# A two-layer hybrid decoder on one core: compressed keys and values in alternating row groups, a norm's weights spread by transpositions, and a new order of the work

## The chip, the core and the metric

The kernel runs on one NeuronCore of a Trainium2 chip. The core has five engines with instruction lists of their own: TensorE (PE in the profile; its weight loads are PEld), VectorE (DVE), ScalarE (ACT), GpSimd (POOL) and SyncE (SP), which here only issues DMAs. The metric is the device time of one execution in microseconds (us). Runs of the kernel before took 556.07, 558.59 and 560.09 us; their median is 558.59.

## What is computed

Two layers of a decoder with 512 tokens and 1024 channels, in float32. Each layer normalises its input, multiplies it by one wide matrix, feeds the columns to four mixers (A: attention on the best 128 keys that an indexer finds; B: attention on compressed, selected and windowed keys with gates; C: a short gated convolution; D: pooling over several windows), gates the results, multiplies them by an output matrix and adds the input. A last normalisation ends it. Cut to what the change touches:

```python
def hybrid_layer(x, norm_w, w_in, w_out, conv_w, pe_cmp, w_cmp_k, w_cmp_v, pool_w, pool_scale):
    h = rmsnorm(x, norm_w)
    p = split_cols(h @ w_in)
    ...
    return x + mixed @ w_out

def compress(tok, w):
    blocks = tok[:, cmp_idx] + pe_cmp
    return blocks.reshape(B, n_cmp, CMP_LEN * HEAD_DIM) @ w

k_cmp = rope(compress(kc_tok, w_cmp_k)[:, :, None], cmp_end, ROT_DIM)[:, :, 0]
v_cmp = compress(vc_tok, w_cmp_v)
```

Compression makes 31 (padded to 32) short keys and values of 64 channels, each from 32 tokens.

## The kernel before

The tokens are four tiles of 128. For the layer's first product, `norm_tile` (line 729) normalises a tile on VectorE, transposes it on TensorE and splits it into a high and a low part (hT, copied by ScalarE and VectorE). Weights come in quarters of 256 rows (`load_w`, line 558): a DMA into a staging tile (st), a cast to the high part (wh) and a subtraction for the low part (wl). A product of hidden state and weights is then three MATMULs per 128 channels (high by high, high by low, low by high), so one tile and one group of columns take 24 (`lin_tok`, line 592). The first group of columns (360) of all four tiles takes 96.

Attention (`probs`, line 995, and `pv`, line 1029) makes scores of four heads on TensorE, takes the smallest on VectorE, exponentials on ScalarE, sums and inverses on VectorE, scales the probabilities on GpSimd, transposes them on TensorE (tr<-ident,pb) and multiplies them by the values.

The work isn't issued as it is written. `record` (line 266) puts every operation on a tape, `cost` (line 318) gives it a duration, the time for which its engine is taken and the time until others see it, and `schedule` (line 388) then builds the five lists: of the operations that could start soonest on an engine it takes the one whose stage has the lowest number in the table RANK (line 195). COLD is the time up to which TensorE's operations are counted double, START the time at which an engine begins. `play` issues the lists; since all instructions are issued by one line of it, the profile names nearly all of them L513, and one goes by the names of the tiles.

Three places matter here.

- The start. `spread` (line 654) multiplies a row of ones with the first norm's weights (g_row, one partition), so that two PSUM banks hold them on all 128 partitions. `warm` (line 646) gives TensorE 40 transpositions of the identity (tr<-ident) that nobody reads; the scheduler uses them as fillers. The loads of the input, the weights and the constants all go through SP's queue.
- `compressed` (line 955) multiplies 32 rows of windows by the weights for keys (s = 0) and then for values (s = 1), 16 products each, into columns 0 to 63 and 64 to 127 of the same 32 partitions of a bank. The profile calls them tr<-st,u. The values' high part is kept in vc on partitions 0 to 31, its low part beside it, and a second copy on 32 to 63.
- The end of layer 0, where the last softmax blocks, the output product and the next layer's normalisation meet.

```python
            pc = bank("tr", 3)
            for s in range(2):
                for t in range(16):
                    PE.matmul(pc[0:32, s * HD : (s + 1) * HD], us[s][:, t::16], wts[2 * s + t // 8][:, t % 8, :],
                              start=t == 0, stop=t == 15)
```

Of the kernel before, what the change touches and what calls it, by code (L numbers as in the profile page):

```python
# [18 lines left out]
P = 128  # L19
T = 512  # L20
NT = T // P
DM = 1024
# [156 lines left out]
class Op:  # L179
    __slots__ = ("eng", "name", "args", "kw", "outs", "ins", "before", "left", "behind", "dur", "occ", "seen",  # L180
                 "tiles", "start", "ready", "num", "locks", "moves", "stage", "rank", "group")


class Engine:
# [9 lines left out]
START = {"PE": 0, "DVE": 0, "ACT": 2070, "POOL": 750, "SP": 800}  # L194
RANK = [
# [28 lines left out]
]  # L224
COLD = 6000


class Tape:
# [1099 lines left out]
```

## Time and profile before

| | |
|---|---|
| runs | 556.07, 558.59, 560.09 us |
| the profiled execution | 558.61 us, its span 556.9 us |
| TensorE busy | 536.8 us of the span |
| VectorE, ScalarE, GpSimd busy | 420.4, 320.4, 294.8 us |
| DMA | 50.62 MB, 91 GB/s over the span |

The span runs from the first to the last instruction; the time holds 1.7 us more. A line of a timeline gives the start in us, the length of the merged piece, the engine, the operation, the tile written <- the tiles read, its shape, how many instructions were merged, and in brackets the idle time of the engine before it with what released it. SPq is the queue of DMAs that SyncE issues. MATMULs are pipelined, so the length of one holds its way through the array, and the distance of two starts says what each costs in a row.

### The profile page before, as it was taken

The page shows a single profiled execution, that of the slowest core. Times are in us where ns is not written, and L with a number is a line of the kernel's source. Part 1 is how long each engine was busy: PE and PEld are TensorE (multiplying, and loading weights), DVE is VectorE, ACT ScalarE, POOL GpSimd, SP SyncE. Part 2 cuts the span into 40 slices and gives each one's busy share as a digit, 9 for nine tenths or more (in the row PEclk, how much of TensorE's full clock was granted, in tenths as well). Part 3 has the DMA queues.
Part 4 walks back from the last instruction along what each step waited for, and adds up shares of the span by engine and source line. Part 5 has one row for each costly group of instructions (what it writes and reads, how often), then busy time and mean ns, then how long its engine had stood idle before and what let it go on. Part 6 is the DMA issues. An engine that isn't in the chain of part 4 may idle for free.

```text
span 556.9 us, 9669 instructions
## 1 busy us (share of the span) xinstructions
PE 536.8 (96%) x3092; PEld 462.2 (83%) x3092; DVE 420.4 (75%) x1152; ACT 320.4 (58%) x797; POOL 294.8 (53%) x399
## 2 busy tenths in 40 slices
PE   8999999999999999899999999999999998999995
PEld 6899987787788778678999999778878876879895
DVE  3837889999998777863256677989999889797623
ACT  4557865443575658563445777555547556776523
POOL 4465743474284746443754666329352583753622
PEclk9999999999999999999999999999999999999998
DMA  8942310583121112106752433148131421030204
GB/s 265 270 127 57 77 39 20 146 202 89 38 76 30 57 39 75 28 2 179 213 156 73 114 92 73 48 111 205 46 87 28 115 55 50 0 106 1 95 1 151
DMA packets 70084, 50.62 MB, mean 91 GB/s; under 512 B 19217, under 2 KB 64401, under 8 KB 70034
## 3 DMA queue, kind: packets, MB, share of 16 engines
q1 hardware_dynamic: 69890, 49.76, 32.5%
q8 instruction: 24, 0.39, 0.3%
q10 hardware_dynamic: 144, 0.26, 0.1%
q14 instruction: 26, 0.21, 0.1%
HBM read 45.81 MB, written 4.19 MB: 90 GB/s over the span
## 4 chain that ended last, share of the span: by engine, by line
PE 75%; DVE 8%; ACT 5%; DMA 4%; POOL 3%; issue 2%; SPq 1%; POOLq 0%; ACTq 0%; DVEq 0%
PE mm L513 56%; PE tr L513 9%; PE s L513 6%; PE pv L513 4%; DMA st<-in_w_in_dram 2%; POOL wl L513 2%; DVE cd L513 2%; SPq L513 1%; DVE acc L513 1%; DVE pb L513 1%; ACT wh L513 1%; DVE pl L513 1%; DMA x<-in_x_dram 1%; ACT qiT L513 1%; ACT rl L513 1%
## 5 line engine op out<-in xcount | busy, mean ns | idle before, releaser
L513 POOL TENSOR_TENSOR wl<-st,wh 128x768 fp32r<-128x768 f32 (+4 forms) x94 | 159.0, 1705 | 77.6 <-ACT wh L513 71.3
L513 PE MATMUL mm<-hT,wh 128*128 128x512 f32 x544 | 179.8, 402 | 1.9 <-ACT wh L513 0.8
L513 PEld LDWEIGHTS mm<-hT,wh 128*128 128x128 f32 x544 | 99.5, 188 | 21.9 <-ACT wh L513 3.8
L513 PE MATMUL mm<-wh,hT 128*128 128x360 f32 (+3 forms) x480 | 104.5, 308 | 0.9 <-ACT z L513 0.9
L513 PE MATMUL mm<-hT,wl 128*128 128x512 f32 x272 | 102.8, 398 | 0.0
L513 POOL TENSOR_SCALAR pb<-pb,rs 128x512 f32<-128x512 f32 (+3 forms) x96 | 55.7, 597 | 78.1 <-DVE rs L513 68.0
L513 ACT ACTIVATE wh<-st 128x768 fp32r<-128x768 f32 (+4 forms) x92 | 71.0, 778 | 40.5 <-PE mm L513 21.8
L513 PE MATMUL mm<-wh,mT 128*128 128x384 f32 (+1 forms) x384 | 92.2, 324 | 1.7 <-ACT wh L513 0.9
L513 PEld LDWEIGHTS mm<-wh,hT 128*128 128x128 f32 x480 | 78.6, 189 | 2.0 <-ACT z L513 1.5
L513 PEld LDWEIGHTS mm<-wh,mT 128*128 128x128 f32 x384 | 66.2, 189 | 5.2 <-ACT wh L513 1.7
L513 PE MATMUL mm<-wl,hT 128*128 128x360 f32 (+3 forms) x240 | 69.8, 307 | 0.3 <-POOL wl L513 0.2
L513 ACT ACTIVATE pb<-pb,mn 128x256 f32<-128x256 f32 (+3 forms) x96 | 53.4, 558 | 25.8 <-DVE mn L513 25.6
L513 PE MATMUL mm<-wl,mT 128*128 128x384 f32 (+1 forms) x192 | 58.8, 323 | 0.0
L513 PEld LDWEIGHTS mm<-hT,wl 128*128 128x128 f32 x272 | 51.0, 188 | 8.9
L513 DVE MAX8 m<-acc 128x8 f32<-128x384 f32 (+2 forms) x96 | 51.7, 551 | 0.5
L513 DVE MATCH_REPLACE8 acc<-m,acc 128x256 f32<-128x256 f32 (+2 forms) x96 | 51.9, 542 | 0.2
L513 ACT ACTIVATE ph<-tr 128x512 fp32r<-128x512 f32 (+1 forms) x68 | 37.7, 593 | 18.8 <-PE tr L513 18.4
L513 DVE TENSOR_TENSOR pl<-tr,ph 128x512 fp32r<-128x512 f32 x60 | 40.2, 684 | 8.3 <-ACT ph L513 7.6
L513 PEld LDWEIGHTS mm<-wl,hT 128*128 128x128 f32 x240 | 44.3, 189 | 1.2 <-POOL wl L513 1.0
L513 PE MATMUL tr<-ident,pb 128*128 128x128 f32 x240 | 44.0, 274 | 1.2 <-POOL pb L513 1.1
L513 DVE CUSTOM_DVE_ANT_0 pb<-s,mask 128x128 f32<-128x128 f32 (+3 forms) x72 | 32.8, 464 | 14.9 <-PE tr L513 7.5
L513 PEld LDWEIGHTS tr<-ident,pb 128*128 128x128 f32 x240 | 30.5, 140 | 11.3 <-POOL pb L513 4.1
(157 smaller groups left out, 898.0 us busy)
## 6 DMA issues: line engine op xcount, KB each, us to landing
st<-in_w_in_dram SPq DMA_DIRECT2D x104, 128.0 KB, 2.6
st<-in_w_in_dram SPq DMA_DIRECT2D x28, 256.0 KB, 3.1
st<-in_w_out_dram SPq DMA_DIRECT2D x16, 384.0 KB, 3.3
x<-in_x_dram SPq DMA_DIRECT2D x16, 256.0 KB, 4.6
st<-in_w_in_dram SPq DMA_DIRECT2D x8, 320.0 KB, 4.6
st<-in_w_out_dram SPq DMA_DIRECT2D x8, 256.0 KB, 2.8
x1d<-x SPq DMA_DIRECT2D x8, 256.0 KB, 4.2
x<-x1d SPq DMA_DIRECT2D x8, 256.0 KB, 3.3
```

The lines of the kernel that those rows point to most:

```text
L513: getattr(self.engines[op.eng].real, op.name)(*[real(a) for a in op.args], **{k: real(v) for k, v in op.kw.items()})
```

## The change

- Keys and values of the compression go to two groups of partitions, 0 to 31 and 32 to 63, in the same columns of one bank, and their products alternate; the weights' loads alternate likewise, and the copies of the values swap their partitions.
- The first norm's weights are loaded as eight rows of 128 by ScalarE's queue, transposed to a column per 128 channels, copied by VectorE, and each column, repeated 128 times, is transposed again into its place in the two banks. The row of ones is gone.
- The scheduler's costs are fitted anew (the landing of a load by rows, TensorE's times, a new time `load` for which a weight load keeps the next TensorE operation away, half the time for products of 32 rows), and writes to one bank by different accumulations wait for one another only where their partitions overlap.
- All ranks are new, COLD is 5600 instead of 6000, ScalarE begins at 800 instead of 2070.

```diff
-START = {"PE": 0, "DVE": 0, "ACT": 2070, "POOL": 750, "SP": 800}
+START = {"PE": 0, "DVE": 0, "ACT": 800, "POOL": 750, "SP": 800}
 RANK = [
-    38, 15, 584, 424, 40, 0, 95, 100, 96, 43, 85, 52, 82, 97, 370, 60, 0, 585, 339, 563, 291, 0, 6, 526, 21, 73,
...
+    583, 29, 585, 581, 518, 0, 283, 160, 177, 3, 101, 151, 129, 145, 507, 102, 0, 68, 584, 582, 532, 0, 74, 105,
...
-COLD = 6000
+COLD = 5600
...
-                    for other in v.tile.groups.values():
-                        if other is not op.group:
+                    for (a, b, _), other in v.tile.groups.items():
+                        if other is not op.group and a < r1 and r0 < b:
                             op.before.update((o.num, o) for o in other)
...
-            op.seen = 2000 + rows * max(run, 512) / 240.0
+            op.seen = 2000 + rows * (2.1 + run / 685.0)
+            if op.eng == "ACT" and not any(o.eng == "ACT" for o in self.ops):
+                op.occ = 1650
         elif op.eng == "PE":
             m = int(np.prod(out.shape[1:]))
+            op.load = 109 * int(np.prod(op.args[1].shape[1:])) / 128
             if op.name == "transpose":
-                op.occ = 108 if m >= 96 else 60
-                op.seen = op.occ + 262
+                op.occ = 60
+                op.seen = 370
...
-                    op.occ = 1.75 * m - 20
+                    op.occ = 1.72 * m + 7
                     op.seen = op.occ + 270
+                    if out.shape[0] == 32:
+                        op.occ *= 0.55
...
+            if e == "PE" and last[e] is not None:
+                s = max(s, last[e].start + op.load * (2 if last[e].start < COLD else 1))
...
-    g_row = res.tile([1, DM], F32, name="g_row", tag="sga")
-    SP.dma_start(g_row, norm_w[0:1, :])
-    ones = res.tile([1, P], F32, name="ones", tag="sgb")
-    G.memset(ones, 1.0)
+    g_row = res.tile([KC, P], F32, name="g_row", tag="sga")
+    S.dma_start(g_row, norm_w[0].rearrange("(k p) -> k p", p=P))
...
     def spread():
+        pg = bank("tr", 3)
+        PE.transpose(pg[:, 0:KC], g_row, ident[0:KC, 0:KC])
+        g_col = res.tile([P, KC], F32, name="g_col", tag="sgb")
+        V.tensor_copy(g_col, pg[:, 0:KC])
         g = [bank("s", 2) for _ in range(2)]
-        for b in range(2):
-            PE.matmul(g[b], ones, g_row[:, half(b)], start=True, stop=True)
+        for k in range(KC):
+            PE.transpose(g[k // 4][:, k % 4 * P : (k % 4 + 1) * P], g_col[:, k : k + 1].to_broadcast([P, P]), ident)
         return g
...
-            for wsrc in (w_cmp_k, w_cmp_v):
-                for q in range(2):
+            for q in range(2):
+                for wsrc in (w_cmp_k, w_cmp_v):
...
-            for s in range(2):
-                for t in range(16):
-                    PE.matmul(pc[0:32, s * HD : (s + 1) * HD], us[s][:, t::16], wts[2 * s + t // 8][:, t % 8, :],
+            for t in range(16):
+                for s in range(2):
+                    PE.matmul(pc[32 * s : 32 * s + 32, 0:HD], us[s][:, t::16], wts[2 * (t // 8) + s][:, t % 8, :],
                               start=t == 0, stop=t == 15)
...
-            S.activation(vc[0:32, 0:HD], pc[0:32, HD:P], AF.Copy)
-            lo(V, vc[0:32, HD:P], pc[0:32, HD:P], vc[0:32, 0:HD])
-            S.activation(vc[32:HD], f(vc[0:32]), AF.Copy)
+            S.activation(vc[32:HD, 0:HD], pc[32:HD, 0:HD], AF.Copy)
+            lo(V, vc[32:HD, HD:P], pc[32:HD, 0:HD], vc[32:HD, 0:HD])
+            S.activation(vc[0:32], f(vc[32:HD]), AF.Copy)
```

What the new order is like shows at three places. First, TensorE's list at the start, in the kernel before (s is the bank with the spread weights, xn a normalised half-tile, tr_94 the fillers):

```order
L513 MATMUL tr_94<-ident 128x128 x16
L513 MATMUL s_154<-g_row,ones 128x512
L513 MATMUL s_168<-g_row,ones 128x512
L513 MATMUL tr_177<-ident,xn_165 128x128 x4
L513 MATMUL tr_94<-ident 128x128 x6
L513 MATMUL tr_199<-ident,xn_184 128x128 x4
L513 MATMUL tr_94<-ident 128x128 x14
L513 MATMUL tr_239<-ident,xn_203 128x128 x4
```

and in the changed kernel (tr_127 are the fillers, tr_125 the small transposition of g_row):

```order
L521 MATMUL tr_125<-ident,g_row 128x8
L521 MATMUL tr_127<-ident 128x128 x3
L521 MATMUL s_141<-ident,g_col 128x128 x4
L521 MATMUL s_157<-ident,g_col 128x128 x4
L521 MATMUL tr_127<-ident 128x128 x6
L521 MATMUL tr_181<-ident,xn_164 128x128 x4
L521 MATMUL tr_127<-ident 128x128
L521 MATMUL tr_191<-ident,xn_174 128x128 x4
L521 MATMUL tr_127<-ident 128x128 x9
L521 MATMUL mm_219<-wh_188,hT_194 128x360 x2
```

The two one-row products are replaced by nine transpositions at the head of the list, the sixteen fillers that stood ahead of them come later, and the first product of hidden state and weights moves ahead of the second tile's transpositions.

Second, SP's queue, in the kernel before (x are half-tiles of the input, st weight quarters in two pieces):

```order
L513 DMA x_79<-in_x_dram 128x512
L513 DMA x_87<-in_x_dram 128x512
L513 DMA g_row<-in_norm_w_dram 1x1024
L513 DMA x_104<-in_x_dram 128x512
L513 DMA x_113<-in_x_dram 128x512
L513 DMA x_121<-in_x_dram 128x512
L513 DMA x_132<-in_x_dram 128x512
L513 DMA st_141<-in_w_in_dram 128x2x320
L513 DMA st_141<-in_w_in_dram 128x2x40
L513 DMA st_152<-in_w_in_dram 128x2x320
L513 DMA st_152<-in_w_in_dram 128x2x40
L513 DMA st_158<-in_w_in_dram 128x2x320
```

and in the changed kernel, where x_81 and x_85 are tile 1, x_92 and x_98 tile 0, x_150 and x_159 tile 3, x_168 and x_178 tile 0 once more for the residual, x_186 and x_197 tile 2, and g_121 half of the next norm's weights:

```order
L521 DMA st_102<-in_w_in_dram 128x2x320
L521 DMA st_102<-in_w_in_dram 128x2x40
L521 DMA g_121<-in_norm_w_dram 128x512
L521 DMA st_137<-in_w_in_dram 128x2x320
L521 DMA st_137<-in_w_in_dram 128x2x40
L521 DMA x_150<-in_x_dram 128x512
L521 DMA x_159<-in_x_dram 128x512
L521 DMA x_168<-in_x_dram 128x512
L521 DMA x_178<-in_x_dram 128x512
L521 DMA x_186<-in_x_dram 128x512
L521 DMA x_197<-in_x_dram 128x512
L521 DMA st_209<-in_w_in_dram 128x2x320
```

The first weight quarter is in fifth place instead of eighth, and the residual's loads stand ahead of tile 2 and of the third quarter. The fourth follows behind one more load. On GpSimd's list the fills and masks of the constants (mask, cbias, cval, pw, u) now stand ahead of the two instructions that make the identity.

Third, TensorE's list at the end of layer 0, where the scores of the last head of group A's third tile (s_2993 in the kernel before) stand thus,

```order
L513 MATMUL s_2993<-kTA_523,qa_601 128x384
L513 MATMUL s_2993<-kTA_551,qa_601 128x384
L513 MATMUL s_3003<-kTA_523,qa_710 128x512
L513 MATMUL pv_2980<-ph_3001,vB_812 128x512
L513 MATMUL s_3003<-kTA_551,qa_710 128x512
L513 MATMUL pv_2980<-pl_3006,vB_812 128x512
L513 MATMUL tr_3017<-ident,pb_2938 128x128
L513 MATMUL tr_3019<-ident,pb_2938 128x128
```

with the block's other ten transpositions behind these two; and in the changed kernel (the last head is s_2950):

```order
L521 MATMUL s_2950<-kTA_496,qa_790 128x384
L521 MATMUL s_2950<-kTA_513,qa_790 128x384
L521 MATMUL s_2963<-kTA_496,qa_662 128x512
L521 MATMUL s_2963<-kTA_513,qa_662 128x512
L521 MATMUL tr_2970<-cd_2896,pw 128x512
L521 MATMUL mm_2883<-wh_2973,mT_2147 128x256
L521 MATMUL mm_2883<-wh_2973,mT_2151 128x256
L521 MATMUL mm_2883<-wh_2973,mT_2147 128x256
L521 MATMUL mm_2883<-wh_2973,mT_2151 128x256
L521 MATMUL tr_2986<-ident,pb_2904 128x128
L521 MATMUL tr_2988<-ident,pb_2904 128x128
L521 MATMUL mm_2990<-wh_2806,mT_2147 128x256
```

The transpositions of the probabilities no longer stand in one row of twelve: they come in groups of two to four with products of the output matrix (mT) between them, and one more score block and the pooling's product stand ahead of them.

## Rows read from the trace of the kernel before

**Rows 1.** The page, busy times by engine and the clock in 40 slices.

```profile
PE 536.8 (96%) x3092; PEld 462.2 (83%) x3092; DVE 420.4 (75%) x1152; ACT 320.4 (58%) x797; POOL 294.8 (53%) x399
...
PEclk9999999999999999999999999999999999999998
```

**Rows 2.** The chain that ended last: its last long piece.

```profile
522.63 28.05 PE mm L513 x190
```

**Rows 3.** Timeline of the start, all engines.

```profile
1.36 0.28 POOL L513 TENSOR_SCALAR_AFFINE_SELECT ident<-ident 128x128 f32<-128x128 f32 x1
...
1.70 3.67 PE L513 MATMUL tr<-ident 128*128 128x128 f32 x16 [1.70 <-POOL ident L513]
...
2.11 0.53 POOL L513 MEMSET mask<- 128x512 f32 x1
...
4.20 0.53 POOL L513 MEMSET pw<- 128x512 f32 x1
...
5.30 3.78 PE L513 MATMUL s<-g_row,ones 1*128 1x512 f32 x4
5.45 0.55 POOL L513 TENSOR_TENSOR ss<-ss,mhalf 128x1 f32<-128x1 f32 x1
...
7.49 0.75 DVE L513 SCALAR_TENSOR_TENSOR xn<-x,ss,s 128x512 f32<-128x512 f32 x1 [7.49 <-PE s L513]
...
8.08 0.63 ACT L513 ACTIVATE junk<-x 128x512 bf16<-128x512 f32 x1 [0.76 <-DMA x<-in_x_dram]
...
9.12 2.07 DVE L513 SCALAR_TENSOR_TENSOR xn<-x,ss,s 128x512 f32<-128x512 f32 x3 [0.88 <-PE s L513]
...
12.05 2.77 PE L513 MATMUL tr<-ident 128*128 128x128 f32 x14
...
14.63 0.90 DVE L513 TENSOR_TENSOR wl<-st,wh 128x720 fp32r<-128x720 f32 x1
14.66 0.60 PE L513 MATMUL tr<-ident,xn 128*128 128x128 f32 x4
...
15.67 0.90 PE L513 MATMUL mm<-wh,hT 128*128 128x360 f32 x4
16.11 0.53 DVE L513 CAST wh<-st 128x720 fp32r<-128x720 f32 x1
...
25.65 0.69 DVE L513 TENSOR_TENSOR hT<-tr,hT 128x512 fp32r<-128x512 f32 x1 [0.47 <-ACT hT L513]
```

**Rows 4.** Timeline of TensorE at the end of the first 96 products.

```profile
34.27 0.33 PE L513 MATMUL mm<-wl,hT 128*128 128x360 f32 x1
34.44 0.49 PE L513 MATMUL mm<-wh,hT 128*128 128x360 f32 x2
34.77 0.33 PE L513 MATMUL mm<-wl,hT 128*128 128x360 f32 x1
34.93 0.93 PE L513 MATMUL mm<-wh,hT 128*128 128x360 f32 x6
```

**Rows 5.** Table of stretches: two of the start, one of layer 0's end.

```profile
core 0: us, PE busy (x) PEld busy (x) DVE busy (x) ACT busy (x) POOL busy (x), PEclk, DMA share, GB/s
0.00:10.00 10.00, 8.30 (x25) 5.43 (x26) 1.63 (x3) 4.88 (x11) 5.93 (x27) 1.00 0.74 236
10.00:20.00 10.00, 10.00 (x64) 9.86 (x63) 8.86 (x14) 4.16 (x9) 2.55 (x3) 1.00 1.10 347
...
226.00:238.00 12.00, 10.44 (x59) 7.35 (x58) 9.77 (x34) 7.35 (x21) 4.26 (x12) 1.00 0.12 31
```

**Rows 6.** Timeline of the end of layer 0.

```profile
234.68 2.27 POOL L513 TENSOR_SCALAR pb<-pb,rs 128x384 f32<-128x384 f32 x4 [2.22 <-DVE rs L513]
...
235.32 2.23 PE L513 MATMUL tr<-ident,pb 128*128 128x128 f32 x12 [0.73 <-POOL pb L513]
```

**Rows 7.** Timeline of the compression in layer 0.

```profile
98.95 3.89 PE L513 MATMUL tr<-st,u 128*32 128x64 f32 x64
```

More of the change, by code (lines that the diff above doesn't have):

```diff
@@ L180 @@
     __slots__ = ("eng", "name", "args", "kw", "outs", "ins", "before", "left", "behind", "dur", "occ", "seen",
-                 "tiles", "start", "ready", "num", "locks", "moves", "stage", "rank", "group")
+                 "tiles", "start", "ready", "num", "locks", "moves", "stage", "rank", "group", "load")
 class Engine:
@@ L325, in cost @@
         op.locks = False
+        op.load = 0.0
         op.moves = op.eng in ("ACT", "DVE") and len({v.region()[0] for v in op.outs[:1] + tensors}) > 1
@@ L342, in cost @@
                 if dt == F32R:
-                    op.occ = max(60, m * 0.426 + 11)
+                    op.occ = m * 0.43 + 12.5
                     op.seen = m * 0.4375 + 205
                 else:
-                    op.occ = 1.75 * m - 20
+                    op.occ = 1.72 * m + 7
                     op.seen = op.occ + 270
+                    if out.shape[0] == 32:
+                        op.occ *= 0.55
             op.dur = op.occ
```

54 rows, old and new, of the table RANK are left out of this document.

## The prediction

> **What bounds the kernel now.** I read the page first: TensorE is busy for 536.8 of 556.9 us and no other engine for more than 75% [rows 1]. The chain of waits ends in one unbroken piece of 190 products on TensorE, 28 us long [rows 2]. So an edit counts if it shortens TensorE's own list, or one of the places where that list stands still. Next I read the table of stretches and then the timeline of three places: the start, the compressed keys, and the end of the first layer.
>
> At the start TensorE looks busy, but with fillers (transpositions of the identity whose result nobody reads). Its first wanted product of hidden state and weights begins at 15.67 and the last of that group's 96 products starts at 34.93 [rows 3]. Products of 360 columns follow one another at 0.165 us (34.27 to 34.93 is four steps) [rows 4], so 96 of them need 15.8 us; the group could be over some microseconds earlier. What holds it is VectorE's list. VectorE begins at 7.49, released by the two one-row products that spread the first norm's weights over the partitions, waits for the second of them until 9.12, and does the last residual (the low part of the hidden state) at 25.65 [rows 3].
>
> At the end of layer 0, from 226 to 238, TensorE is idle for 12.00 - 10.44 = 1.56 us [rows 5], and the twelve transpositions at 235.32 take 2.23 us, in step with GpSimd's four scalings of the probabilities (2.27 us) [rows 6].
>
> **The change, part by part.**
>
> *Spread of the norm's weights.* Gone: four MATMULs with one row, 3.78 us on TensorE [rows 3], and the 4 KB load that stood third in SP's queue. New: a load of eight rows from ScalarE's queue, one transposition, a copy of eight columns on VectorE, eight transpositions of a column repeated 128 times. Early transpositions take 3.67 us for sixteen, 0.23 each [rows 3], so the eight cost 1.8 us where 3.78 stood. But TensorE's first instruction now waits for that load and for the identity, and everything on TensorE is queued behind it. GpSimd makes the identity by 1.64 in the kernel before; in the new order the constants that took it from 2.11 to 4.73 (2.6 us) stand ahead, so I put the identity at 4.2. The load, if it takes as long as the old one (issued at 1.72, used at 5.30, so 3.6 us) and is issued at 0.8, is there at 4.4. From there: transposition and copy to 5.0 (three fillers cover them), first half of the weights at 6.0, second at 6.9. The row scale is ready at 6.0 as before (5.45 + 0.55) [rows 3]. So VectorE's first normalisation starts at 6.1, not 7.49, and the second at 6.9, not 9.12.
>
> *Order of the loads.* Tile 1 of the input now comes first, then tile 0, then the first weight quarter in fifth place, where the fifth half-tile was read at 8.08 [rows 3]; I take 8.2 for it. Behind it the residual's norm row (0.26 MB) and tile 0 of the residual (0.52 MB) are drawn ahead of tile 2 and of the last two weight quarters. By bytes: 2.36 MB are in by 10 us and 0.347 MB per us follow [rows 5]. Tile 2 ends at 3.6 MB, that is 13.6; the third weight quarter at 4.0 MB, 14.7; the last (behind another 0.26 MB) at 4.6 MB, 16.5. In the kernel before the last quarter ended at 3.7 MB, 13.9. So the loads cost 2.6 us more for the last quarter and cover for it is VectorE's list, as follows.
>
> *VectorE's list.* It holds the same work: 8 normalisations of 0.75, 4 casts of 0.53, 8 residuals of 0.69, 2 weight residuals of 0.90, 15.4 us together [rows 3]. From 7.49 to 26.34 it had 18.85 us, so 3.4 us were waits. From 6.1, with half a microsecond lost to the first weight quarter and some 0.9 elsewhere, the list ends at 22.9. Then two of the four tiles are still to be multiplied: 48 x 0.165 = 7.9 and three transpositions of 0.15 (four took 0.60 at 14.66 [rows 3]), so the group ends at 31.2 at best, against 35.1. The fillers stand in TensorE's list ahead of wanted work (nine before the first product, five before the third tile), and can cost up to 0.8; I take 32.0, a gain of **3.1 us**. Ends: 4.5, if VectorE loses nothing; 0, if the late loads are really what ends last.
>
> *Compressed keys and values.* 32 products per layer, two MATMULs each, take 3.89 us in a row with nothing idle inside [rows 7], 0.06 us per MATMUL; both layers 7.8. Now keys go to partitions 0 to 31 and values to 32 to 63 of the same bank, turn by turn. The trace of before shows no two accumulations side by side in different columns of the array. If they don't overlap, the gain is 0. If they do, the time halves at best, 3.9 us for both layers. I take **3.3 us**, near the upper end, for it is one or the other: a product's own two passes stay one behind the other, and only the other group's fill the gap. The copies behind them are the same in number and size; the keys' copy, which could start before the values were done, now starts with them, but TensorE has other work there.
> [...]
>
> *New ranks and costs.* These reorder all engines. At the end of layer 0 the old list puts four instructions between the last scores of a softmax block and the transpositions of its probabilities, and then all twelve of these in a row; the new one puts seven there, and products between the transpositions. Of the idle 1.56 us and the stretch of the twelve (2.23 - 12 x 0.15 = 0.4) I take 1.5 as regained. For other places I take nothing: they may gain as much again in layer 1, or lose it. Ends: 5 gained, 6 lost (three bare blocks as priced under D).
>
> **Sum.** 3.1 + 3.3 + 1.5 = 7.9. The profiled execution took 558.6 us (span 556.9 and 1.7 around it), the median of the three runs is the same 558.6, so the forecast is 550.7, said as **551 us**.
>
> **The rivals.**
> *B, no overlap of the two groups.* For: no row shows one, and rows share the bank. Against: the groups use other columns and other partitions. Time 551 + 3.3 = 554.3.
> *C, the start gains nothing.* Either loads end last (0.78 MB of early residual at 0.347 per us is 2.2 us, and tile 2 and both late quarters stand behind it), or TensorE's clock is still at its lower level when the products begin at some 11.5 instead of 15.67 (the cast at 8.2, one more normalisation and the first tile's two residuals end near 10.5 on VectorE, and the nine fillers go on for a microsecond more). [...] Twenty products at double step cost 20 x 0.165 = 3.3. Time 551 + 3.1 = 554.1, and 557.4 with B.
> [...]
> *D, slower.* The ranks were refitted for estimates, and the new list may leave softmax blocks bare as the one at 234 was: TensorE waits there until GpSimd, itself 2.22 us idle for the row sums, has scaled [rows 6]. A bare block costs 1.56 idle and 0.4 of stretch, 2.0. The kernel has 24 such blocks (two layers, four tiles, one of group A and two of group B). From seven more bare ones on it decides: 551 + 14 = 565. For: two new places at the start of layer 1, where z is transposed with little in between. Against: the blocks I looked at have more work between, not less.
>
> **How the numbers follow.** About 1% (5.6 us) is what a measurement of this kernel can tell from no change: faster is below 553.0, slower above 564.2. Chances: the forecast 0.55 (545 to 555 by itself), B 0.15, C 0.18, D 0.12. Of the forecast's 0.55 some 0.46 lie below 553.0; B and C add 0.08 where the order gains more than I took; so faster 0.54, same 0.36, slower 0.10. The range goes from all upper ends (4.5 + 3.9 + 5 = 13.4, 545) with a little beyond, 543.5, to B and C with some of D, 561.
>
> **What would show it.** Right: the first normalisation on VectorE near 6.1, the last residual of the start near 23, the last of the 96 products near 32; the 64 MATMULs of a compression in some 2.2 us; TensorE busy by some 5 us less in sum; less idle between 220 and 240. Wrong: 3.9 us for the 64 (B); ScalarE or VectorE idle for a DMA between 12 and 18, or products at 0.3 us near 12 (C); new idle of TensorE behind GpSimd's scalings anywhere (D).

## The result: 554.9 us, half a per cent faster where 1.4% was forecast

The changed kernel takes 554.88 us (median of 20 runs, 553.49 to 558.16), the kernel before beside it 558.28 (20 runs, 555.76 to 560.11): a ratio of 0.9949, 95% interval 0.9931 to 0.9966, or 2.8 us (1.9 to 3.9; the two medians differ by 3.4, inside that interval). It is faster, but within the 1% that the forecast called no change, and the gain is well under half of the 7.9 us that were summed. The range held it; it lies where rivals B and C put it (554.3, 554.1), but neither of their mechanisms is what happened. Of the executions that follow, many differ by when TensorE's clock rises (4.8 to 14.2 us into the span) or falls (to 0.50, at a cost of 1.7 us of full clock); no comparison here can be understood without that, and it is shown below.

The page of the changed kernel: busy times by engine, and the clock in 40 slices.

```profile
PE 530.8 (96%) x3097; PEld 457.0 (82%) x3097; DVE 423.3 (76%) x1153; ACT 318.2 (57%) x797; POOL 297.8 (54%) x398
...
PEclk9999999999999999999999999989999999999998
```

TensorE is busy for 6.0 us less than in [rows 1], and its span is 2.9 us shorter (554.0 against 556.9): so it is idle for 23.2 us instead of 20.1. One slice of the clock has an 8 that [rows 1] has not.

The timeline of the start, what answers to [rows 3] and [rows 4]:

```profile
3.90 0.27 PE L521 MATMUL tr<-ident,g_row 8*128 8x8 f32 x1 [3.90 <-POOL ident L521]
...
4.79 1.92 PE L521 MATMUL s<-ident,g_col 128*128 128x128 f32 x8
...
6.39 1.41 DVE L521 SCALAR_TENSOR_TENSOR xn<-x,ss,s 128x512 f32<-128x512 f32 x2 [2.02 <-POOL ss L521]
...
9.57 0.59 PE L521 MATMUL mm<-wh,hT 128*128 128x360 f32 x2
...
22.45 0.69 DVE L521 TENSOR_TENSOR hT<-tr,hT 128x512 fp32r<-128x512 f32 x1 [0.32 <-ACT hT L521]
...
31.86 0.45 PE L521 MATMUL mm<-wh,hT 128*128 128x360 f32 x2
32.15 0.28 PE L521 MATMUL mm<-wl,hT 128*128 128x256 f32 x1
```

VectorE's first normalisation starts at 6.39 (forecast 6.1), its last residual of the start at 22.45 (near 23), and the last product of the 96 at 31.86 (32.0), against 34.93. TensorE from the compression of layer 1 on, what answers to [rows 7], and the clock there (table of stretches, columns as in [rows 5]):

```profile
363.85 2.17 PE L521 MATMUL tr<-st,u 128*32 128x64 f32 x64
365.95 0.50 PE L521 MATMUL s<-kiT,qiT 96*128 96x512 f32 x1
366.29 0.60 PE L521 MATMUL tr<-ident,z 128*128 128x128 f32 x4
367.08 0.44 PE L521 MATMUL tr<-ident,z 128*128 128x128 f32 x2 [0.19 <-DVE vc L521]
367.27 0.49 PE L521 MATMUL s<-kiT,qiT 96*128 96x512 f32 x1
369.11 2.79 PE L521 MATMUL mm<-hT,wh 128*128 128x512 f32 x6 [1.34 <-ACT wh L521]
```

```profile
220.00:240.00 20.00, 18.68 (x119) 15.98 (x118) 16.87 (x42) 14.03 (x35) 9.32 (x17) 1.00 0.11 31
...
368.00:370.00 2.00, 0.89 (x3) 0.69 (x4) 1.97 (x6) 2.00 (x5) 0.86 (x1) 0.83 0.85 243
370.00:372.00 2.00, 2.00 (x6) 1.62 (x5) 1.96 (x5) 1.90 (x5) 2.00 (x2) 0.50 0.31 71
372.00:374.00 2.00, 2.00 (x8) 1.57 (x8) 1.91 (x5) 0.11 (x1) 2.00 (x3) 0.82 0.95 224
```

The 64 MATMULs take 2.17 us instead of 3.89, as forecast. But behind them TensorE stands still for 1.34 us, until ScalarE has cast the gate's first weights, and then its clock is at the lower level for a while: (1 - 0.83) x 2 + (1 - 0.50) x 2 + (1 - 0.82) x 2 = 1.7 us of full clock are lost.

So every sign of being right came (TensorE is idle for 1.3 us from 220 to 240, where it was 1.9), and of the signs of being wrong a part of D's: TensorE's idle time in front of the transpositions of probabilities is 2.3 us in sum instead of 1.2. The time did not come. To see where it went, a yardstick: each form of MATMUL counts for its usual step from start to start (the lower quartile of its steps gives this table to within 0.3 us), with fillers, the spread and the compression left out, and the table says at what time of its span each execution has got through so many us of that work. It counts TensorE's work alone and is rough where the mix of forms differs. Two executions of either kernel are in it (the second ones are from the runs b_same and a_same below).

```
work done (us)       20     60     80    100    180    200    300    320    460
before            35.88  82.67 108.51 129.68 221.75 251.02 359.24 385.36 546.38
before, second    32.46  79.37 105.31 126.31 218.06 247.33 355.36 381.51 543.31
changed           32.80  80.00 104.46 128.48 221.89 247.83 357.50 384.18 543.52
changed, second   32.18  79.54 103.68 127.70 220.91 246.89 356.53 381.87 541.11
```

Against the profile on which the forecast rested the changed kernel is 3.1 us ahead at the start; against another execution of the kernel before it is 0.3 us behind. And the two kernels change the lead several times after that.

### The profile page after: what moved, and what is told of

It is laid out like the page before. It is cut to its first block, busy times and chain, and to the rows that moved or that the text cites. A ratio compares the mean times of both kernels' runs of the same rounds, so it can differ in the third digit from the quotient of the medians.

```text
span 554.0 us, 9676 instructions
## 1 busy us (share of the span) xinstructions
PE 530.8 (96%) x3097; PEld 457.0 (82%) x3097; DVE 423.3 (76%) x1153; ACT 318.2 (57%) x797; POOL 297.8 (54%) x398
## 4 chain that ended last, share of the span: by engine, by line
PE 80%; DVE 6%; ACT 5%; DMA 3%; POOL 3%; issue 2%; SPq 0%; POOLq 0%; ACTq 0%; DVEq 0%
PE mm L521 58%; PE tr L521 10%; PE s L521 7%; PE pv L521 5%; POOL wl L521 2%; DMA st<-in_w_in_dram 1%; ACT wh L521 1%; DVE acc L521 1%; DVE pb L521 1%; DMA x<-in_x_dram 1%; DMA st<-in_w_out_dram 1%; DVE om L521 1%; POOL pb L521 1%; ACT rl L521 1%; DVE pl L521 0%
## 5 line engine op out<-in xcount | busy, mean ns | idle before, releaser
L521 PE MATMUL mm<-wl,hT 128*128 128x360 f32 (+3 forms) x240 | 68.3, 306 | 0.0
L521 ACT ACTIVATE pb<-pb,mn 128x128 f32<-128x128 f32 (+3 forms) x96 | 53.5, 558 | 25.2 <-DVE mn L521 24.8
L521 DVE MAX8 m<-acc 128x8 f32<-128x256 f32 (+2 forms) x96 | 51.9, 551 | 0.8
L521 DVE MATCH_REPLACE8 acc<-m,acc 128x384 f32<-128x384 f32 (+2 forms) x96 | 51.8, 541 | 0.1
```

Of the source, the lines that this page charges most:

```text
L521: getattr(self.engines[op.eng].real, op.name)(*[real(a) for a in op.args], **{k: real(v) for k, v in op.kw.items()})
```

## The experiments

In all of them each engine's list is held fixed: the order that the planner found for the kernel before (the old list), or for the changed one (the changed list), is written out, so that an edit moves nothing else. Each list was thus planned for the work of its own kernel, and an edit in the other's list stands where no planner has placed it. Ratios are to the kernel before on the same chip (its median was 557.2 to 557.8 us in these sets), with their 95% intervals.

### What the compression's gain runs into

**a_noalt**: the changed kernel's list, keys' products ahead of the values' on the same partitions (the copies behind them, not shown here, go with it).

```diff
-            for t in range(16):
-                for s in range(2):
-                    PE.matmul(pc[32 * s : 32 * s + 32, 0:HD], ...
+            for s in range(2):
+                for t in range(16):
+                    PE.matmul(pc[0:32, s * HD : (s + 1) * HD], ...
```

> The changed kernel with its list of instructions held fixed, but the compressed keys' sixteen products stand ahead of the values' sixteen again, on the same 32 partitions. Ring theory (in layer 1 the next projection's weights cannot be loaded until the compression frees the four staging buffers, and TensorE's clock falls in that wait): layer 0 loses 1.7 us; in layer 1 the wait of 1.5 us before the gate's first product goes and the 3.2 us at half clock (1.6 us) with it, so 1.7 lost and about 3 regained; in sum 554 to 556 us, within 1 us of the changed kernel. Order theory (the faster compression is worth its whole 3.3 us and the new list of instructions lost them elsewhere): 554.9 + 3.3 = 558.2 us.

Measured: 556.31 us, ratio 0.9993 (0.9980 to 1.0006), so 0.44% (2.4 us) is lost against the changed kernel. TensorE in layer 1:

```profile
363.76 3.89 PE L635 MATMUL tr<-st,u 128*32 128x64 f32 x64
...
370.61 2.92 PE L635 MATMUL mm<-hT,wh 128*128 128x512 f32 x6 [1.35 <-ACT wh L635]
```

Neither theory holds. The wait is 1.35 us behind the slow compression as well as 1.34 behind the fast one: the alternation did not make it. From the compression's first MATMUL to the gate's first product it is 370.61 - 363.76 = 6.85 us here and 369.11 - 363.85 = 5.26 in the changed kernel, so in this place 1.6 of the 1.7 us saved are kept.

**b_alt**: the list of before, with the alternation alone (the edit of a_noalt the other way round).

> The kernel before with its list held fixed; only the compressed products take turns on two groups of 32 partitions. Ring theory: 1.7 us gained in layer 0, where scores follow that wait for no weights; nothing in layer 1, where the gate's first product still starts about 371.5 less what layer 0 gained, with 1.7 us more idle before it; if the clock falls in that wait, another 1.6 us lost: 556.6 to 558.2 us. Order theory: the full 3.3 us, 555.0 us. In either case 64 MATMULs in some 2.2 us instead of 3.89.

Measured: 556.10 us, ratio 0.9976 (0.9955 to 0.9996): 1.3 us (0.2 to 2.5), less than the full 3.3. The two kernels of the same list at layer 0's compression, the alternating one first, then the kernel before:

```profile
95.44 2.20 PE L627 MATMUL tr<-st,u 128*32 128x64 f32 x64
97.58 1.20 PE L627 MATMUL s<-kTB,qb 128*128 128x512 f32 x4
100.31 0.50 PE L627 MATMUL s<-kTB,qb 128*128 128x512 f32 x1 [1.54 <-DVE mn L627]
```

```profile
102.78 1.20 PE L513 MATMUL s<-kTB,qb 128*128 128x512 f32 x4
104.40 0.50 PE L513 MATMUL s<-kTB,qb 128*128 128x512 f32 x1 [0.42 <-DVE mn L513]
```

From the compression's first MATMUL to the fifth score it was 104.40 - 98.95 = 5.45 us [rows 7] and is 100.31 - 95.44 = 4.87. Of 1.7 us saved, 1.1 are waited again, for VectorE to take the row maxima (mn) from the scores. By the yardstick, against the second execution of the kernel before, the alternation is worth 0.4 us in layer 0 and 0.85 in layer 1, where the waits for ScalarE behind it grew from 0.25 and 0.29 us to 0.37, 0.78 and 0.28.

**a_own**: the compression's weights in a space of their own, so that the gate's weights find their buffers free.

```diff
+            space = res.tile([P, 4, 8, HD], F32, name=nm("wc"), tag="mT0")
...
-                    wt = wp.tile([P, 8, HD], F32, name=nm("st"), tag="st", bufs=4)
+                    wt = space[:, len(wts)]
```

> The changed kernel with its list held fixed; the compression's weights lie in the space that the mixed tile takes later, so the next projection's weights find the four staging buffers free. Ring theory: the 1.5 us of idle before the gate's first product in layer 1 and the 1.6 us of half clock behind it go: 551.8 us (551 to 553). Order theory: that place is not what holds the kernel, 554.9 us, within 0.7 us.

Measured: 553.64 us, ratio 0.9948 (0.9930 to 0.9967), the changed kernel's 0.9949. The loads of the gate's first weights are now issued by 351.5 us, where they were issued from 365.1 on, and the wait is the same. TensorE, then ScalarE:

```profile
367.92 2.50 PE L635 MATMUL mm<-hT,wh 128*128 128x512 f32 x6 [1.34 <-ACT wh L635]
```

```profile
364.90 0.27 ACT L635 ACTIVATE zc<-tr 32x128 f32<-32x128 f32 x1 [1.54 <-PE tr L635]
365.19 0.21 ACT L635 ACTIVATE vc<-tr 32x64 fp32r<-32x64 f32 x1
365.43 0.60 ACT L635 ACTIVATE rl<-s 128x512 f32<-128x512 f32 x1
365.92 0.76 ACT L635 ACTIVATE qb<-tr 64x256 fp32r<-64x256 f32 x2
366.70 0.38 ACT L635 ACTIVATE kTB<-tr 128x256 fp32r<-128x256 f32 x1
366.98 0.36 ACT L635 ACTIVATE qb<-tr 64x256 fp32r<-64x256 f32 x1
367.25 0.62 ACT L635 ACTIVATE wh<-st 128x512 fp32r<-128x512 f32 x1
```

The buffers were not what held it. The cast (wh) stands in ScalarE's list behind seven instructions, the first of which waits for the compression; in the changed kernel the load and this list merely ended together.

**a_own_early**: as a_own, with the gate's first two casts moved ahead of those copies in ScalarE's list, and GpSimd's two subtractions with them.

> The changed kernel with the compression's weights in a space of their own and, in layer 1, the first two casts of the gate's weights (and GpSimd's two subtractions behind them) moved ahead of the copies of the compressed keys in ScalarE's list. ScalarE theory (with the buffers free, the wait of 1.34 us for the gate's first weights is ScalarE's list, where six copies stand ahead of the cast): the wait falls below 0.4 us, the clock has no reason to fall behind it, 552.3 us (551.5 to 553) against 553.9 for the changed kernel. Rival (VectorE, busy for 97% of that stretch, takes back what TensorE gains): wait gone, time 553.4 to 554.

Measured: 553.79 us, ratio 0.9945 (0.9923 to 0.9967): nothing gained. TensorE there:

```profile
366.63 0.44 PE L635 MATMUL tr<-ident,z 128*128 128x128 f32 x2 [1.30 <-DVE vc L635]
...
369.95 1.89 PE L635 MATMUL mm<-hT,wh 128*128 128x512 f32 x7 [0.80 <-ACT wh L635]
```

The wait has moved: now TensorE's transpositions wait for VectorE to empty the compression's bank (vc), and its products for the third cast. VectorE is busy for 19.4 of the 20 us from 360 to 380 here, as in the changed kernel's second profile. The rival's time came, though not its "wait gone". That VectorE takes the gain in this place fits these rows; no run with less work on VectorE was made in the changed list.

**b_half and b_alt_half**: the list of before without and with the alternation, VectorE's top-k cut to half its rounds (these kernels leave out half of the selection).

```diff
-            for _ in range(TOPK // 8):
+            for _ in range(TOPK // 16):
```

> The kernel before with its list held fixed, but only 8 of the 16 rounds of each top-k (the selection is left out in half, so the masks differ): VectorE has 0.9 us less to do per round and tile. The measure for the next. VectorE theory (from 80 to 165 and from 345 to 470 VectorE's list, 95 to 99% busy, ends the waits of TensorE behind it): several us less than the kernel before, 550 to 555 us. TensorE theory (TensorE alone bounds those stretches): within 1 us of the kernel before.

> As the one before it, with the compressed products taking turns on two groups of 32 partitions. VectorE theory: relieved of half the top-k, TensorE keeps what the alternation saves: between the same two places of the list 1.7 us per layer less than in its partner (with the full top-k the traces show 0.5 in layer 0 and 0.8 in layer 1). Rival (something else holds TensorE behind the compression, such as the scores' two banks or the loads): again about 0.5 and 0.8.

Measured: 556.02 us, 0.9973 (0.9955 to 0.9990), and 552.60 us, 0.9914 (0.9890 to 0.9939). The fifth score in the two:

```profile
103.81 0.50 PE L625 MATMUL s<-kTB,qb 128*128 128x512 f32 x1 [0.43 <-DVE mn L625]
```

```profile
101.21 0.49 PE L625 MATMUL s<-kTB,qb 128*128 128x512 f32 x1 [0.80 <-DVE mn L625]
```

With the compressions starting at 98.36 and 97.15, it is 5.45 and 4.06 us to the fifth score: 1.4 of the 1.7 us are kept there, where 0.6 were with the whole top-k. So it is VectorE's list that takes the gain at that place. By the times the alternation is now worth 0.6% (3.3 us, uncertain by 1.7), its whole size; by the yardstick, in the two profiled executions, still 0.4 us at 100 us of work and another 1.1 in layer 1. What makes the rest in the times is not settled. That VectorE's top-k bounds the kernel by itself is not so: halving it gave 0.27% (1.5 us), less than the VectorE theory said and more than the other allowed.

### What the clock does

**b_same and a_same**: both kernels with their lists written out and nothing changed, for a second profile and as a measure.

> The kernel before with its list written out and nothing changed: a second profile of it. Clock theory (in some executions of the kernel before TensorE's clock rises only near 14.3 us, in others near 6.5 us, and the 96 products of the start end near 34.9 or near 31.3 accordingly; the profile on which the forecast rested was one of the late ones): one of these two ends, nothing between, and times spread from 555.5 to 560.5 us. Fixed-cost theory (the late end is what the loads and the one-row products cost in every execution): 34.9 again.

> The changed kernel with its list written out and nothing changed, as the measure for the others of this set and a second profile of it. The 96 products end between 31.4 and 31.9 as in four profiles so far; times 553.5 to 556 us, median 554.3 to 554.9. If the fall of the clock behind the wait at 368 is not in every execution, this profile may be without it, and then ends some 1.6 us earlier.

Measured: 556.74 us, ratio 1.0001 (0.9975 to 1.0027), and 553.88 us, 0.9942 (0.9919 to 0.9964). The second profile of the kernel before, at the start and in layer 1:

```profile
1.70 3.67 PE L627 MATMUL tr<-ident 128*128 128x128 f32 x16 [1.70 <-POOL ident L627]
5.30 2.01 PE L627 MATMUL s<-g_row,ones 1*128 1x512 f32 x4
```

```profile
456.00:458.00 2.00, 0.48 (x3) 0.09 (x1) 2.00 (x8) 1.40 (x4) 0.29 (x1) 1.00 0.26 67
458.00:460.00 2.00, 1.90 (x6) 1.28 (x7) 1.80 (x6) 1.51 (x4) 1.31 (x3) 0.84 0.19 64
460.00:462.00 2.00, 2.00 (x7) 1.58 (x7) 2.00 (x4) 0.42 (x1) 2.00 (x3) 0.50 0.00 0
462.00:464.00 2.00, 2.00 (x8) 1.18 (x8) 1.45 (x3) 0.16 (x1) 0.60 (x1) 0.80 0.21 18
```

The same four one-row MATMULs that took 3.78 us in [rows 3] take 2.01: here the clock rose at 5.4 us, there at 14.2 (the first record of the granted clock in each trace; ahead of it the view prints 1.00, and the step between transpositions tells the level: in the first profile 213 ns up to 14.18 us, 109 from 14.33 on). The last of the 96 products starts at 31.50 instead of 34.93. The forecast's basis was an execution with a late rise. Later, after TensorE waited for most of 456 to 458, the clock fell as it does in the changed kernel at 369; the changed kernel's second profile has its wait of 1.34 us too, but no fall behind it.

**b_newg and a_oldg**: the spread alone, new in the old list and old in the changed list. The load of the weights is on ScalarE's queue in both.

```diff
-            PE.matmul(g[b], ones, g_row[:, half(b)], start=True, stop=True)
+            PE.transpose(g[k // 4][:, ...], g_col[:, k : k + 1].to_broadcast([P, P]), ident)
```

> The kernel before with its list held fixed; only the first norm's weights are spread by transpositions of a column instead of the one-row products, from a load on ScalarE's queue. Clock theory with the one-row products as its cause: the clock rises before 11 us in every execution, the 96 products end near 31.3, no time above 558, median 556.0 us against 557.2 to 558.3 of the kernel before. Rival (the spread sets when VectorE starts): VectorE's first normalisation no earlier than 6.9, so no gain that way, and the late executions stay: median 557 to 558, up to 560.4.

> The changed kernel with its list held fixed; the one-row products spread the first norm's weights again, from a contiguous 4 KB load on ScalarE's queue. Clock theory: executions with a late rise come back, a part of the times is 2 to 3.5 us longer, median 555.5 to 557 us, and the profile shows the 96 products ending at 31.5 or at 34 to 35. Rival (only the second half of the weights comes later, 7.7 instead of 7.1): 0.6 us at most, all times within 553.5 to 556.5 us, median 555 us.

Measured: b_newg 556.43 us, 0.9983 (0.9962 to 1.0004), no time over 557.8; a_oldg 556.76 us, 0.9993 (0.9973 to 1.0014), so 0.5% (2.9 us, uncertain by 1.7) worse than a_same. The rise came at 5.8 us in b_newg's profile and at 12.4 in a_oldg's, whose 96th product starts at 33.21. In b_newg it starts at 32.57, not at the 31.3 expected: in the old list ScalarE there waits for a half-tile of the input until 7.85, which it has at 6.78 in b_same, and the first wanted product starts at 12.88 instead of 11.81. So in this list the new spread costs 1.1 us against an execution with an early rise; the times near 560 that the kernel before has are gone.

**b_fullrow**: the kernel before; the four MATMULs keep form, place and result, but have 128 rows, 127 of them zeros.

```diff
-    g_row = res.tile([1, DM], F32, name="g_row", tag="sga")
-    SP.dma_start(g_row, norm_w[0:1, :])
-    ones = res.tile([1, P], F32, name="ones", tag="sgb")
+    g_row = res.tile([P, DM], F32, name="g_row", tag="sga")
+    V.memset(g_row, 0.0)
+    SP.dma_start(g_row[0:1], norm_w[0:1, :])
+    ones = res.tile([P, P], F32, name="ones", tag="sgb")
```

> The kernel before with its list held fixed; the four MATMULs that spread the first norm's weights have 128 rows instead of one (the row and 127 rows of zeros, which VectorE clears first), with the same columns, place and result. One-row theory (products with one row do not keep TensorE's clock up or bring it up): the clock rises by 6.5 us and stays, the 96 products end near 31.5 in every execution, no time above 558, median 556.0 us. Rival (their form or the place is the reason, or chance alone): late executions as before, times up to 560 us, median 557 to 558.

Measured: 556.06 us, ratio 0.9977 (0.9959 to 0.9995); one time of twelve at 558.1, the others below 557.4, where ten of 23 of the kernel before on the same chip lay above 558. The 96th product starts at 31.86. The profile:

```profile
5.18 2.29 PE L628 MATMUL s<-g_row,ones 128*128 128x512 f32 x4
```

Zeros that add nothing make the kernel 0.23% faster. Together with the profiles this bears the one-row theory out: in the seven profiles with one-row products the rise came at 4.8, 5.4 and 6.1, or at 12.4, 12.6, 13.0 and 14.2, and in the one that rose at 4.8 (b_alt_half) the clock was at the lower level again from 8.2, behind the one-row products, until 11.6. In the nine without them it came between 5.8 and 10.1.

**a_fill**: twelve unused transpositions ahead of the gate's first product of layer 1, in the changed kernel's list.

```diff
+        for _ in range(fill):
+            PE.transpose(ps[:, :P], ident, ident)
```

> The changed kernel with its list held fixed and twelve unused transpositions of the identity put ahead of the gate's first product of layer 1, where TensorE stands idle for 1.34 us. If the clock fell because TensorE stood idle, and transpositions count as work for it, the granted clock stays 1.00 from 369 to 373 and 1.6 us are gained: 553.3 us. If transpositions do not count, or the clock falls for another reason, the clock falls to 0.5 as before and the time is 554.9 us or up to 0.3 us more.

Measured: 553.84 us, ratio 0.9942 (0.9922 to 0.9961), with the changed kernel's 0.9949 and 0.9942 no difference. The stretch that had 0.83 and 0.50:

```profile
368.00:370.00 2.00, 1.90 (x15) 1.70 (x15) 1.97 (x8) 1.96 (x7) 0.00 (x0) 1.00 1.03 318
370.00:372.00 2.00, 1.97 (x10) 1.39 (x8) 1.97 (x6) 1.95 (x5) 1.83 (x2) 1.00 0.43 148
```

The clock stays up over the wait. But of the six profiles of the changed list with this wait three have the fall (the changed kernel, a_noalt, a_own) and three do not (a_same, a_oldg, a_order), so one profile without it does not show that the transpositions held the clock. This profile has its fall elsewhere, where the other profiles of the changed list have none: the granted clock is 0.61 and 0.54 in the two stretches from 228 to 232, behind waits of 0.42 and 0.77 us. The expected 1.6 us were not gained; whether the transpositions prevent the fall stays open.

### How the parts add up

**a_order**: the changed kernel's list with both edits undone (those of a_noalt and a_oldg together): the new order alone.

> The changed kernel's list of instructions with both of its edits of the work undone (one-row products for the first norm's weights, keys' products ahead of the values'): the new order alone. If the three parts add up (changed kernel 0.54% under the one before; undoing the spread gives back 0.5%, undoing the alternation 0.45%), the new order alone is 0.4% slower than the kernel before: 559 to 560 us. If it is worth nothing either way: the time of the kernel before, 556.7 to 558. If it is worth the 1.5 us that the forecast gave it: 555 to 556.5.

**b_alt_newg**: the list of before with both edits (those of b_alt and b_newg).

> The kernel before with its list held fixed and both edits of the work: the compressed products take turns, and the first norm's weights are spread by transpositions. If the two add up as measured one by one (0.24% and 0.17%), 0.41% less than the kernel before, some 555.2 us, and the new list with its loads is worth 0.15% more. If the new list gains nothing at all beside them: 0.55% less, 554.5 us. If they do not add up in the old list: 556 us.

Measured: a_order 558.22 us, 1.0017 (0.9999 to 1.0035); b_alt_newg 556.54 us, 0.9985 (0.9968 to 1.0002). All eight corners, as the change of time against the kernel before (each uncertain by about 0.2):

```
                     no edit   alternation   spread    both
list of before          0        -0.24%      -0.17%   -0.15%
changed list         +0.17%      -0.07%      -0.07%   -0.51% and -0.58%
```

The new list alone gains nothing and may lose up to 2 us; the edits alone in the old list give 0.8 us. Together they give 2.8 to 3.2. So the parts do not add. Put on the kernel before one at a time, the alternation, the spread and the list give 1.3, 0.9 and -0.9 us. Taken from the changed kernel one at a time, they cost 2.4 to 2.8 (a_noalt), 2.5 to 2.9 (a_oldg) and 2.0 to 2.4 us (b_alt_newg), each uncertain by 1.2 to 1.7. A list planned for the fast compression and the new spread, and without worth for the old ones, would look like this; that it is the reason is not shown.

In the profile of b_alt_newg one loss can be seen: against b_newg it is 1.9 us ahead at 310 us of work and 0.4 from 400 on. In between lies the long wait near layer 1's end (1.57 us in the kernel before), and behind it the clock falls (0.64 and 0.51 in the two stretches from 460 to 464), as it does in four of the eight profiles of the old list, with either edit or none. That explains this one execution, not the median of twelve. The changed list has no such wait there, and no fall there in any of its profiles.

## Why the forecast was wrong, step by step

**What bounds the kernel.** "An edit counts if it shortens TensorE's own list" is the step on which the miss rests first. TensorE is busy for 96%, but VectorE nearly is too where the edits lie. I read its share over the whole span, 75%. Two stretches of the kernel before, then one of the changed kernel's second profile (the columns are those of [rows 5], VectorE is DVE; the changed kernel's first profile has 18.50 there):

```profile
80.00:100.00 20.00, 19.78 (x105) 15.91 (x104) 18.91 (x44) 11.79 (x24) 5.50 (x7) 1.00 0.12 27
140.00:160.00 20.00, 19.92 (x103) 15.72 (x101) 19.78 (x45) 11.71 (x23) 10.06 (x9) 1.00 0.11 26
```

```profile
360.00:380.00 20.00, 18.48 (x136) 14.35 (x135) 19.40 (x56) 9.86 (x20) 12.83 (x9) 1.00 0.61 157
```

In such a stretch the shortened list of one engine waits for the other. At one place this is shown: with half the top-k on VectorE the gain up to layer 0's fifth score went from 0.6 to 1.4 us of 1.7.

**Compressed keys and values: the size on TensorE right, the worth wrong.** 64 MATMULs in 2.17 us where 2.2 was said, 1.7 us less in layer 1 (as in layer 0 of b_alt, 2.20), 3.89 / 2.17 = 1.8 times as fast: so rival B fell, and the two groups overlap although they share a bank. But 3.3 us arrive nowhere with the whole top-k: 1.3 in the old list (b_alt), 1.35 in the changed list with the old spread (a_order to a_oldg), 2.4 to 2.8 in the changed kernel itself (a_noalt). The step that failed is "TensorE has other work there". In layer 0 its scores wait for VectorE, and by the yardstick 0.3 to 1.1 of the 1.7 us are left at 100 us of work, in either list. In layer 1 the old list gives half of them to waits for ScalarE and keeps 0.85; the changed list keeps 1.6.

**New ranks and costs: not a term that can be added.** At layer 0's end products now stand between the transpositions, the wait of 0.73 us for GpSimd is gone, and from 180 to 200 us of work the changed kernel takes 25.9 us where 29.3 stood: 3.3 us, more than the 1.5 booked. But "for other places I take nothing" left out what the same list loses elsewhere: 4.2 us from 80 to 180 us of work (117.4 against 113.2 in the first profiles) and 1.5 from 200 to 300 (109.7 against 108.2), of which 1.7 come back from 320 to 460. The gain at layer 0's end and the loss ahead of it are in part the same work moved. VectorE is busy for 17.7 us in the stretch from 180 to 200 where it was 21.7, and by its start it has been busy for 182.3 us where it was 177.0. So the place that I priced was not a gain by itself. Alone the list is worth -0.9 us (-1.9 to 0.1) instead of +1.5; behind both edits it is worth 2.0 to 2.4. A part of rival D's mechanism is in it: the waits for GpSimd that rose from 1.2 to 2.3 us, 0.94 of them at 114.8.

**The start: 3.1 us forecast, 2.5 to 2.9 measured in the changed list (a_oldg), for another reason.** The three landmarks came to within 0.6 us, but most of what the old start lost was not VectorE's order and the loads. It was the clock: where it rises early the old start's 96 products end at 31.5 too. The step that failed is taking a single profile's slow transpositions at 12.05 [rows 3] for a property of the kernel; the second half of rival C saw the lower clock and looked for it in the new kernel alone, whose rise (7.5 us) came ahead of its first product (9.57), so that no product of its start ran at the double step (transpositions: 213 ns up to 7.35 us, 109 from 7.53 on). That the worth came near the forecast is luck in part: against an early execution the new start gains nothing, and the spread alone is worth 0.9 us in the old list. The clock also rose with transpositions alone on TensorE: at 7.5 us in the changed kernel, where nothing else had run there since 3.90, and between 7.6 and 10.1 in five more profiles with the same start, each ahead of the first product.

**The sum.** The step that carries the miss is 3.1 + 3.3 + 1.5, three terms added as if each came on top of the others: 2.8 and 3.2 us were measured for the three together. Along one path (the list, then the alternation, then the spread) the worths are -0.9, 1.35 and 2.85; along another (the alternation, the spread, the list) 1.3, -0.5 and 2.0 to 2.4. Each path ends at the measured gain by construction, and no path gives the terms that I booked. How the 4.6 us that are missing divide among the three therefore stays open. The second profiles of the two kernels, both with an early rise, differ by 2.2 us at 460 us of work, and 1.7 of these are the fall behind 459 in the kernel before: in that pair little is left but the clock.

## What to carry to other kernels

Before an engine's saving is booked, look at every other engine's share of that very stretch: behind work that two engines share, a saving on one can turn into a wait for the other (1.1 of 1.7 us in layer 0 of b_alt), and here freeing the buffer or moving the cast that the wait named only showed the next one (1.34 us in a_own, 1.30 and 0.80 in a_own_early). Do not add savings that were forecast or measured one by one: here three that cost 2 to 3 us each when taken away gave 3 us together. Before a profile's start is taken as the kernel's, take a second profile: one execution here differed from another of the same list by 3.4 us at the end of the start. And where one-row products stand before the first real work, try them with rows of zeros, or transpositions: here the zeros took 0.23% off (0.05 to 0.41), and with the transpositions in the old list no time lay over 557.8, where the kernel before on the same chip had times up to 560.5.

## What the runs showed of the hardware

- With one-row products before the first real work TensorE's clock rose at 12.4 to 14.2 us in four profiles of seven and at 4.8 to 6.1 in three, without them at 5.8 to 10.1 in all nine; with 127 rows of zeros added it came at 6.0 in the one profile, and the time fell by 0.23% (0.05 to 0.41).
- Behind a wait of 1.3 to 1.6 us in the middle of full work the granted clock fell to 0.50, costing 1.7 us of full clock, in seven profiles of the fifteen with such a wait in layer 1. At the start the granted clock's row reads 1.00 while transpositions run at double step (213 ns from start to start in the kernel before up to 14.18 us, 109 from 14.33 on): the step tells the clock there, the row does not.
- Two accumulations into partitions 0 to 31 and 32 to 63 of one bank, their products by turns, overlapped: 34 ns for each MATMUL of 64 columns (2.17 us for 64) instead of 61 (3.89) on the same partitions, one accumulation behind the other.
